# Two encoder layers on one core: products of probabilities placed one projection or a gate later, and the ring of PSUM banks begun at bank 7

## The chip, the cores and the metric

The kernel runs on one core of one Trainium2 chip. The metric is device time in microseconds (us) of one execution. The kernel before takes 1705.44 us, the median of 3 runs (1705.37 to 1705.56). PE is TensorE, DVE is VectorE, ACT is ScalarE, SP is SyncE, which issues the loads of the weights; PSUM has 8 banks of 128 x 512 floats here, named 0 to 7.

## The reference

An encoder of two layers over 512 tokens of 1024 channels in float32. Each layer computes

```
h = rmsnorm(x);  z = h @ w_in          # q, k, v of three mixers, and three gates
y_na  = neighbourhood attention of z   # 8 heads of 64, window 8 x 16 on a 64-wide grid
y_mla = latent attention of z          # 4 heads
y_gqa = windowed grouped attention     # 8 heads, 2 key heads, window 128, a sink logit
x = x + (sum_i sigmoid(gate_i) * (y_i @ w_br_i)) @ w_out
x = x + conv_ffn(rmsnorm(x))           # up to 2 x 2816, conv of width 3, gelu, down
```

and a last rmsnorm follows. Every attention is scores, softmax, and the product of the probabilities with the values.

## The kernel before, in words

Activations are held as [channel, token] tiles of 128 x 512. A float32 product is made of three fp32r matmuls: each operand is split into a high part (a cast by ACT, line 153) and a low part (the rest, by DVE, line 154), and `mm3` (lines 162 to 169) adds high x high, low x high and high x low. A projection of the 1024 channels (`dense`, line 171) is 8 x 3 = 24 matmuls of 128 x 512, a branch product (`do_br`, line 730) 4 x 3 = 12.

The order of PE and of SP is written out by hand: `schedule` (line 274) returns a list of items, and `run` (line 337) emits them one after the other. DVE and ACT are ordered by the framework's scheduler, which puts splits of weights and softmax work ahead by a priority. The engines take their instructions in that order. The items that matter here, `p` being a pair of heads, `h` a head, `i` a block of 128 queries of one key head:

- `("naq", p)`, `("nak", p)`, `("nav", p)`: projections for q, k, v of neighbourhood attention (24 matmuls each). `("nvt", p)` transposes v (4 matmuls, line 642).
- `("ns", p)`: scores of two heads into 4 banks; DVE adds the bias (line 674), finds maxima (line 677), ACT takes the exponential (line 679), DVE scales (line 682). `("nt", p)`: 32 small transposes of the probabilities into 4 banks (line 234), from which ACT casts `ph` and DVE subtracts `pl` (`unfold`, line 237). `("np", h)` (line 692): 8 matmuls of 256 columns of one head's `ph` and `pl` with the values (line 702); ACT and DVE then take the result from its bank (lines 706, 708).
- `("gs", i)`, `("gt", i)`, `("gp", i)`: the same three steps of the grouped-query mixer. The scores are masked by DVE (line 817); a block has 2 or 3 key blocks, so `gp` (lines 856 and 857) is 4 or 6 matmuls of 512 columns. There is a single pair of `ph` and `pl` buffers here.
- `gate()`: the next gate, 24 matmuls, evacuated by DVE into a `gz` tile (line 160; 5 buffers, line 39) and by ACT's tanh (line 718). `("br", b, m)`: a branch product, 12 matmuls, whose bank and gate DVE merges (lines 738, 740, 741).

The weights come as `raw` tiles (3 buffers, loaded by SP, line 118) and are split into `whi` and `wlo` (3 buffers each). When an item takes its weights, the split of the item two further on is emitted (`weights`, line 141), so that it starts when the item before has given its buffer back: a gate's weights are 128 x 1024, a branch product's 128 x 512.

Between the latent attention and the output projection all items take their banks in turn from one ring of eight (`do_mla_attn`, line 521, sets it; `bank`, line 104, hands them out). One layer takes 203 banks from it. Then `do_out` (line 871) sets groups: the first four output products run in banks 2, 3, 4, 5, the next in 6, 7, 0, 1.

Of the kernel before, what the change touches and what calls it, by code (L numbers as in the profile page):

```python
# [59 lines left out]
class Trunk:  # L60
# [213 lines left out]
    def schedule(self, l):  # L274
        d = self.d
        w_in, w_uq, w_ukv = d["w_in"][l], d["w_uq"][l], d["w_ukv"][l]
        W = {}
        halves = lambda w, cs: [(w, 512 * hf, 4, c, P) for hf in range(2) for c in cs]
        W["lat"] = halves(w_in, [OFF_CQ + i * P for i in LAT])
        if l == 0:  # L280
            W["lat"][:4] = [(w_in, k * P, 1, OFF_CQ, 4 * P) for k in range(4)]
        W["lat4"] = [(w_in, 0, KD, OFF_CQ + 4 * P, P)]
        W["kr"] = [(w_in, 0, KD, OFF_KR, 64)]
        W["v", 0] = [(w_ukv, 0, 2, 512, 512)]
        W["qr"] = [(w_uq, 0, 3, 512, 256)]
        for h in range(4):
            W["qn", h] = [(w_uq, 0, 3, h * P, P)]
            W["kn", h] = [(w_ukv, 0, 2, h * P, P)]
        for p in range(4):
            for i, n in enumerate("qkv"):  # L290
                W["na" + n, p] = [(w_in, 0, KD, 512 * i + p * P, P)]
        W["gk"] = [(w_in, 0, KD, OFF_GK, P)]
        W["gv"] = [(w_in, 0, KD, OFF_GV, P)]
        for i in range(4):
            W["gq", i] = [(w_in, 0, KD, OFF_GQ + i * P, P)]
        for b in range(3):
            for m in range(KD):
                W["gate", b, m] = [(w_in, 0, KD, OFF_GATE + b * D + m * P, P)]
                W["br", b, m] = [(d["w_br"][b][l], 0, 4, m * P, P)]
        W["br012"] = W["br", 2, 0] + W["br", 2, 1] + W["br", 2, 2]  # L300
        W["out"] = halves(d["w_out"][l], [m * P for m in range(4)])
        for m in range(4, KD):
            W["out", m] = [(d["w_out"][l], 0, KD, m * P, P)]
        ups = [p * NF + f for f in range(NF) for p in range(2)]
        W["up"] = halves(d["w_up"][l], [f * P for f in ups[:4]])
        for f in ups[4:]:
            W["up", f] = [(d["w_up"][l], 0, KD, f * P, P)]
        for g in range(2):
            W["down", g] = [(d["w_down"][l], k0 * P, nk, (4 * g + m) * P, P)
                            for k0, nk in ((0, 8), (8, 8), (16, 6)) for m in range(4)]  # L310

        gate = iter([("gate", b, m) for b in (1, 0, 2) for m in range(8)]).__next__
        s = ["mla_open", "lat", "qr", "lat4", "rs_q", "kr", gate(), "rs_k", ("qn", 0), ("v", 0), ("v", 1), "rb_k"]
        s += [("kn", 0), gate(), "mla_attn", ("qn", 1), ("kn", 1), ("mr", 0), ("ms", 0), gate()]
        for h in range(3):
            s += [("mt", h), ("mr", h + 1), ("ms", h + 1)]
            s += [("qn", h + 2), ("kn", h + 2)] if h < 2 else [("naq", 0)]
            s += [("mp", h)] + ([gate()] if h == 1 else [])
        s += [("nak", 0), ("mt", 3), gate(), ("nav", 0), ("mp", 3), "na_open", ("nvt", 0), ("ns", 0)]
        s += [("naq", 1), ("nak", 1), ("br", 1, 0), gate(), ("ns", 1), ("nt", 0)]  # L320
        s += [("nav", 1), ("np", 0), ("np", 1), ("naq", 2), ("nvt", 1), ("nak", 2), ("br", 1, 1), gate(), ("ns", 2), ("nt", 1)]
        s += [("nav", 2), ("np", 2), ("np", 3), ("naq", 3), ("nvt", 2), ("nak", 3), ("br", 1, 2), gate(), ("ns", 3), ("nt", 2)]
        s += [("nav", 3), ("np", 4), ("np", 5), ("br", 1, 3), gate(), ("nvt", 3), ("br", 1, 4), gate(), ("br", 1, 5), ("nt", 3)]
        s += [("br", 1, 6), gate(), ("np", 6), ("np", 7), ("br", 1, 7)]
        s += ["gq_open", "gk", ("gq", 0), "gv", ("gq", 1), "gvt", gate(), ("gs", 0), ("br", 0, 0), ("gq", 2), ("br", 0, 1), ("gq", 3)]
        for i in range(7):
            s += [("gs", i + 1), ("gt", i), ("br", 0, i + 1) if i else gate(), ("gp", i), gate()]
        s += [("gt", 7), gate(), ("gp", 7), "br012", ("br", 2, 3)]
        for m in range(4, 7):
            s += [gate(), ("br", 2, m)]  # L330
        s += [("br", 2, 7)]
        s += ["out"] + [("out", m) for m in range(4, KD)]
        s += ["up"] + [("up", f) for f in ups[4:]]
        s += [("down", 0), ("down", 1)]
        return s, W
# [183 lines left out]
            self.qr.append((own, other))  # L519

    def do_mla_attn(self):
        self.banks(ring=list(range(8)))

    def do_qn(self, h):
        ps = self.dense(self.spec(), self.lat[:3])
# [593 lines left out]
```

## Time and profile before

| | us |
|---|---|
| median of 3 runs | 1705.44 |
| the profiled execution | 1705.71 |
| its span, first to last instruction | 1703.9 |
| PE busy | 1684.3 |
| DVE busy | 1119.9 |
| ACT busy | 829.6 |
| PE's waits that the list of waits names | 14.4 |

The first layer's neighbourhood section lies at about 138 to 265 us of the span, its grouped-query section at 294 to 407, its output projection begins at 446; in the second layer the same sections lie at 982 to 1108, 1139 to 1251, and 1290 us. A row of the timeline reads: start, duration, engine, line, operation, tile written <- tiles read, size, count, and in brackets how long the engine had been idle before it and who ended that. A matmul's row lasts until the modelled end of its pipeline, so rows of matmuls that follow each other closely overlap: how fast they follow is read from their starts.

### The profile page before, as it was taken

Reading aid. Unit: us, or ns where it says so; the run is one execution under the profiler, and the core shown is the slowest. Engines: PE = TensorE matmul, PEld = TensorE weight load, DVE = VectorE, ACT = ScalarE, POOL = GpSimd, SP = SyncE. Lnnn points to the kernel's source line nnn. Section 1 sums busy time; section 2 is a strip of 40 time slices with the busy share of each in tenths; the row PEclk is TensorE's granted clock in tenths of the full one; section 3 lists DMA queues with packets and bytes.
Section 4 is the critical chain, followed back from the end, with each engine's and each line's share of the span. In section 5 each row is a group of like instructions: output and inputs, shape, how many; then the busy total and the mean of one; then the engine's idle time right before and its main releaser. Section 6 shows DMA issues by size and latency. Waiting matters only on the chain.

```text
span 1703.9 us, 22124 instructions
## 1 busy us (share of the span) xinstructions
PE 1684.3 (99%) x8466; PEld 1386.8 (81%) x8466; DVE 1119.9 (66%) x1845; ACT 829.6 (49%) x1461; POOL 52.2 (3%) x107
## 2 busy tenths in 40 slices
PE   9999999999999999999999999999999999999998
PEld 8887788878888888888887887887788888888887
DVE  7777766786558777734367687668766587777234
ACT  7654445675435444433266554467644444444232
POOL 1110000000000000000011100000000000000000
PEclk9999999999999999999999999999999999999999
DMA  6233223222324333323232323322223333333231
GB/s 183 68 102 85 78 84 88 74 69 75 105 83 116 98 100 99 99 87 101 80 96 80 96 75 84 90 81 69 64 79 105 99 112 98 93 94 99 87 105 68
DMA packets 289401, 155.44 MB, mean 91 GB/s; under 512 B 8880, under 2 KB 285376, under 8 KB 289296
## 3 DMA queue, kind: packets, MB, share of 16 engines
q1 hardware_dynamic: 286752, 148.88, 30.5%
q0 software_dynamic: 2256, 4.83, 0.9%
q8 instruction: 66, 1.08, 0.3%
q14 instruction: 39, 0.32, 0.1%
q10 hardware_dynamic: 288, 0.33, 0.1%
HBM read 151.89 MB, written 2.10 MB: 90 GB/s over the span
## 4 chain that ended last, share of the span: by engine, by line
PE 93%; DVE 5%; ACT 1%; issue 1%; DMA 0%; ACTq 0%
PE ps_ring L167 12%; PE ps_ring L168 11%; PE ps_ring L169 11%; PE ps_d L169 11%; PE ps_d L168 11%; PE ps_d L167 11%; PE ps_g L167 7%; PE ps_g L168 7%; PE ps_g L169 7%; DVE pl L154 1%; PE ps_ring L247 1%; PE ps_ring L234 1%; DVE wlo L154 1%; PE ps_ring L857 1%; PE ps_ring L702 1%; PE ps_g L267 1%
## 5 line engine op out<-in xcount | busy, mean ns | idle before, releaser
L153 ACT CAST whi<-raw 128x1024 fp32r<-128x1024 f32 (+4 forms) x339 | 301.0, 888 | 603.5 <-PE ps_g L168 190.5
L154 DVE TENSOR_TENSOR wlo<-raw,whi 128x1024 fp32r<-128x1024 f32 (+4 forms) x337 | 344.5, 1022 | 187.3 <-ACT whi L153 185.8
L169 PE MATMUL ps_d<-hh,wlo 128*128 128x512 f32 x685 | 266.7, 389 | 0.0
L168 PE MATMUL ps_d<-hl,whi 128*128 128x512 f32 x685 | 266.5, 389 | 0.0
L167 PE MATMUL ps_d<-hh,whi 128*128 128x512 f32 x685 | 266.5, 389 | 0.0
L167 PE MATMUL ps_ring<-hh,whi 128*128 128x512 f32 x600 | 234.8, 391 | 0.6 <-DVE pt L674 0.6
L169 PE MATMUL ps_ring<-hh,wlo 128*128 128x512 f32 x600 | 233.7, 389 | 0.0
L168 PE MATMUL ps_ring<-hl,whi 128*128 128x512 f32 x600 | 233.6, 389 | 0.0
L169 PEld LDWEIGHTS ps_d<-hh,wlo 128*128 128x128 f32 x685 | 128.6, 188 | 27.1 <-DVE wlo L154 0.6
L168 PEld LDWEIGHTS ps_d<-hl,whi 128*128 128x128 f32 x685 | 128.6, 188 | 26.7
L167 PEld LDWEIGHTS ps_d<-hh,whi 128*128 128x128 f32 x685 | 128.6, 188 | 26.6
L167 PEld LDWEIGHTS ps_ring<-hh,whi 128*128 128x128 f32 x600 | 112.7, 188 | 24.6 <-DVE pt L674 1.0
L169 PEld LDWEIGHTS ps_ring<-hh,wlo 128*128 128x128 f32 x600 | 112.6, 188 | 23.8
L168 PEld LDWEIGHTS ps_ring<-hl,whi 128*128 128x128 f32 x600 | 112.7, 188 | 23.2
L169 PE MATMUL ps_g<-ff,wlo 128*128 128x512 f32 x334 | 129.9, 389 | 0.0
L167 PE MATMUL ps_g<-ff,whi 128*128 128x512 f32 x334 | 129.9, 389 | 0.0
L168 PE MATMUL ps_g<-ff,whi 128*128 128x512 f32 x334 | 129.9, 389 | 0.0
L160 DVE TENSOR_TENSOR u<-ps_d,rb 128x512 f32<-128x512 f32 x80 | 55.2, 690 | 63.2 <-PE ps_d L169 63.2
L160 DVE TENSOR_TENSOR gz<-ps_ring,rb 128x512 f32<-128x512 f32 x44 | 30.4, 691 | 94.9 <-PE ps_ring L169 94.9
L167 PEld LDWEIGHTS ps_g<-ff,whi 128*128 128x128 f32 x334 | 62.7, 188 | 13.1
L169 PEld LDWEIGHTS ps_g<-ff,wlo 128*128 128x128 f32 x334 | 62.7, 188 | 13.0
L168 PEld LDWEIGHTS ps_g<-ff,whi 128*128 128x128 f32 x334 | 62.7, 188 | 12.9
(331 smaller groups left out, 2864.3 us busy)
## 6 DMA issues: line engine op xcount, KB each, us to landing
raw<-in_w_in_dram SPq DMA_DIRECT2D x86, 512.0 KB, 3.9
raw<-in_w_up_dram SPq DMA_DIRECT2D x80, 512.0 KB, 3.7
raw<-in_w_down_dram SPq DMA_DIRECT2D x32, 512.0 KB, 3.8
raw<-in_w_down_dram SPq DMA_DIRECT2D x16, 384.0 KB, 3.4
raw<-in_w_in_dram SPq DMA_DIRECT2D x17, 256.0 KB, 2.8
raw<-in_w_br_mla_dram SPq DMA_DIRECT2D x16, 256.0 KB, 2.7
raw<-in_w_br_na_dram SPq DMA_DIRECT2D x16, 256.0 KB, 2.7
raw<-in_w_br_gqa_dram SPq DMA_DIRECT2D x16, 256.0 KB, 2.8
```

Source lines behind the costliest of these rows:

```text
L153: nc.scalar.copy(hi, src)
L154: nc.vector.tensor_sub(lo, src, r32(hi))
L160: self.nc.vector.tensor_tensor(out, a, b, ALU.mult)
L167: mm(ps, sh, mh, start=first and k == 0, stop=False)
L168: mm(ps, sh, ml, start=False, stop=False)
L169: mm(ps, sl, mh, start=False, stop=last and k == n - 1)
L234: self.nc.tensor.transpose(out[i][:, n * 64:n * 64 + 64], block[q], self.idf[q, q])
L247: self.nc.tensor.matmul(out, st[a], mv[b], start=first and t == 0, stop=last and t == 2)
L267: self.nc.tensor.matmul(self.gbank[j], w[:, j * P:(j + 1) * P], m, start=n + t == 0, stop=False)
L702: nc.tensor.matmul(pq[:, qs], self.vs[p][:, ch, j, :], pm[:].rearrange("p (k c) -> p k c", c=P)[:, ks], start=i == 0 and m == 0, stop=i == ...
L857: nc.tensor.matmul(po, self.gvs[:, k0 + kb, g, :], pl, start=False, stop=kb == nk - 1)
```

## The change

Three things are changed: the place of `np` in the neighbourhood rows, the place of `gp` in the grouped-query loop, and the first bank of the ring.

```diff
-        s += [("nav", 1), ("np", 0), ("np", 1), ("naq", 2), ("nvt", 1), ("nak", 2), ("br", 1, 1), gate(), ("ns", 2), ("nt", 1)]
+        s += [("nav", 1), ("naq", 2), ("np", 0), ("np", 1), ("nvt", 1), ("nak", 2), ("br", 1, 1), gate(), ("ns", 2), ("nt", 1)]
...
-        s += [("nav", 3), ("np", 4), ("np", 5), ("br", 1, 3), gate(), ("nvt", 3), ("br", 1, 4), gate(), ("br", 1, 5), ("nt", 3)]
+        s += [("nav", 3), ("br", 1, 3), ("np", 4), ("np", 5), ("nvt", 3), gate(), ("br", 1, 4), gate(), ("br", 1, 5), ("nt", 3)]
...
-            s += [("gs", i + 1), ("gt", i), ("br", 0, i + 1) if i else gate(), ("gp", i), gate()]
+            s += [("gs", i + 1), ("gt", i), gate(), ("gp", i), ("br", 0, i + 1) if i else gate()]
...
     def do_mla_attn(self):
-        self.banks(ring=list(range(8)))
+        self.banks(ring=[7, 0, 1, 2, 3, 4, 5, 6])
```

The row that begins with `("nav", 2)` is changed like the first one: `("naq", 3)` goes ahead of `("np", 2)` and `("np", 3)`. For `i = 0` the loop's order stays as it was, with a gate on both sides of `gp`. The number of banks taken from the ring is the same 203.

On PE, in the first layer's loop at `i = 4`, behind the scores of block 5 and the transposes of block 4, a branch product stood ahead of `gp`; before:

```order
L247 MATMUL ps_ring<-gk,gq 128x384 x12
L234 MATMUL ps_ring<-idf,pt 128x64 x16
L167 MATMUL ps_ring<-ynh_1925,whi 128x512
L168 MATMUL ps_ring<-ynl_1926,whi 128x512
L169 MATMUL ps_ring<-ynh_1925,wlo 128x512
```

and now:

```order
L247 MATMUL ps_ring<-gk,gq 128x384 x12
L234 MATMUL ps_ring<-idf,pt 128x64 x16
L167 MATMUL ps_ring<-h_102,whi 128x512
L168 MATMUL ps_ring<-h_103,whi 128x512
L169 MATMUL ps_ring<-h_102,wlo 128x512
```

The tiles `ynh` and `ynl` are the neighbourhood mixer's output, which the branch product reads; `h` is the normed input, which the gate reads. The 12 matmuls between the transposes and `gp` have become 24, and the 12 now stand between `gp` and the next scores.

On DVE, at the same place, the queue behind PE's last item before the scores of block 5 (a gate before, a branch product now) up to the masked scores (`pt_3834` to `pt_3849`); before:

```order
L160 TENSOR_TENSOR gz_3814<-ps_ring_3789,rb_327 128x512
L154 TENSOR_TENSOR wlo_3885<-raw_3882,whi_3884 128x512
L817 ISA pt_3834,nm_3817<-ps_ring_3818,gmask_99,nsink_2875 128x384
L817 ISA nm_3817 128x1
L817 ISA pt_3837,nm_3817<-ps_ring_3819,gmask_99,nsink_2875 128x384
L817 ISA nm_3817 128x1
L817 ISA pt_3846,nm_3817<-ps_ring_3826,gmask_99,nsink_2875 128x384
L817 ISA nm_3817 128x1
L817 ISA pt_3849,nm_3817<-ps_ring_3827,gmask_99,nsink_2875 128x384
```

and now:

```order
L740 SCALAR_TENSOR_TENSOR gz_3357<-gz_3357,ps_ring_3802 128x512
L154 TENSOR_TENSOR yal0_3789<-yf_3360,yah0_3788 128x512
L741 TENSOR_TENSOR mg4_2656<-mg4_2656,gz_3357 128x512
L817 ISA pt_3834,nm_3817<-ps_ring_3818,gmask_99,nsink_2875 128x384
L817 ISA nm_3817 128x1
L817 ISA pt_3837,nm_3817<-ps_ring_3819,gmask_99,nsink_2875 128x384
L817 ISA nm_3817 128x1
L154 TENSOR_TENSOR wlo_3885<-raw_3882,whi_3884 128x1024
L817 ISA pt_3846,nm_3817<-ps_ring_3826,gmask_99,nsink_2875 128x384
L817 ISA nm_3817 128x1
L154 TENSOR_TENSOR yal1_3793<-yf_3360,yah1_3792 128x512
L817 ISA pt_3849,nm_3817<-ps_ring_3827,gmask_99,nsink_2875 128x384
```

In place of a gate's evacuation and a narrow `wlo` there stand the two instructions of a merge, a wide `wlo`, and (in this pass alone) the low parts `yal` of two finished output tiles. The two `pl` subtractions follow right behind the last row now; before, three small softmax instructions stood between.

On DVE in the neighbourhood section, behind the scaling of the probabilities of `("ns", 1)` (`pt_1810` is the last), the difference reads:

```order
 L682 TENSOR_SCALAR pt_1810<-pt_1810,nm_1812 128x256 x2
-L708 TENSOR_TENSOR yf_1541<-ps_ring_1913,tt_1922 64x4x8x16
-L154 TENSOR_TENSOR ynl0_1926<-yf_1541,ynh0_1925 128x512
-L160 TENSOR_TENSOR ev_1960<-ps_ring_1935,rb_327 128x512
+L160 TENSOR_TENSOR ev_1932<-ps_ring_1907,rb_327 128x512
 L154 TENSOR_TENSOR wlo_1978<-raw_1975,whi_1977 128x1024
+L154 TENSOR_TENSOR nq_1935<-ev_1932,nq_1934 128x512
+L708 TENSOR_TENSOR yf_1541<-ps_ring_1950,tt_1959 64x4x8x16
 L154 TENSOR_TENSOR vs_1966<-ps_ring_1967,vs_1966 128x8x64
-L154 TENSOR_TENSOR nq_1963<-ev_1960,nq_1962 128x512
+L708 TENSOR_TENSOR yf_1541<-ps_ring_1938,tt_1947 64x4x8x16
+L154 TENSOR_TENSOR ynl0_1963<-yf_1541,ynh0_1962 128x512
```

The evacuation (`ev`) and split (`nq`) of the next q projection have moved ahead of the evacuation (`yf`) of the two `np` products and of the split of their sum.

More of the change, by code (lines that the diff above doesn't have):

```diff
@@ L320, in schedule @@
         s += [("naq", 1), ("nak", 1), ("br", 1, 0), gate(), ("ns", 1), ("nt", 0)]
-        s += [("nav", 1), ("np", 0), ("np", 1), ("naq", 2), ("nvt", 1), ("nak", 2), ("br", 1, 1), gate(), ("ns", 2), ("nt", 1)]
-        s += [("nav", 2), ("np", 2), ("np", 3), ("naq", 3), ("nvt", 2), ("nak", 3), ("br", 1, 2), gate(), ("ns", 3), ("nt", 2)]
-        s += [("nav", 3), ("np", 4), ("np", 5), ("br", 1, 3), gate(), ("nvt", 3), ("br", 1, 4), gate(), ("br", 1, 5), ("nt", 3)]
+        s += [("nav", 1), ("naq", 2), ("np", 0), ("np", 1), ("nvt", 1), ("nak", 2), ("br", 1, 1), gate(), ("ns", 2), ("nt", 1)]
+        s += [("nav", 2), ("naq", 3), ("np", 2), ("np", 3), ("nvt", 2), ("nak", 3), ("br", 1, 2), gate(), ("ns", 3), ("nt", 2)]
+        s += [("nav", 3), ("br", 1, 3), ("np", 4), ("np", 5), ("nvt", 3), gate(), ("br", 1, 4), gate(), ("br", 1, 5), ("nt", 3)]
         s += [("br", 1, 6), gate(), ("np", 6), ("np", 7), ("br", 1, 7)]
```

## The prediction

> **What bounds the kernel now.** I read the page first, then PE's list of waits, then the timeline at each wait, of PE and of the engine waited for.
>
> ```profile
> span 1703.9 us, 22124 instructions
> PE 1684.3 (99%) x8466; PEld 1386.8 (81%) x8466; DVE 1119.9 (66%) x1845; ACT 829.6 (49%) x1461; POOL 52.2 (3%) x107
> ```
>
> PE is busy for 99% of the span, so nothing but PE's stalls can be won, some 20 us at most. The profiled execution took 1705.71 us, 1.8 us more than its span and 0.27 us more than the median of the runs, 1705.44. Terms come from the profiled one and are taken off the median. PE's waits, in us in total, times, and the longest:
>
> ```profile
> PE ps_ring L702 <- DVE pl L154: 5.8, 4, 1.4
> PE ps_ring L857 <- DVE pl L154: 3.8, 10, 0.6
> PE ps_g L167 <- DVE gz L740: 1.7, 2, 0.9
> PE ps_ring L167 <- DVE pt L674: 1.2, 6, 0.2
> ```
>
> The first two are products of probabilities that wait for DVE's low part `pl`: line 702 in neighbourhood attention, line 857 in the grouped-query loop. The third is the first output product, which waits for DVE to empty a bank. The three come to 11.3 us, and the change touches each. The fourth is the bank of the first projection behind `nt`; that projection keeps its place and its bank's history, so I leave it.
>
> These figures are idle time behind a matmul's modelled end, and a stall costs more. So I price each stall by whole sections, from first start to next start, against the same section where nothing waits.
>
> **Neighbourhood rows.** The stalled pair of `np` in the first layer, then a pair that has no stall:
>
> ```profile
> 167.85 0.28 PE L702 MATMUL ps_ring<-ph,vs 128*128 128x256 f32 x1
> 170.57 0.39 PE L702 MATMUL ps_ring<-pl,vs 128*128 128x256 f32 x1 [1.45 <-DVE pl L154]
> 171.50 0.39 PE L167 MATMUL ps_ring<-h,whi 128*128 128x512 f32 x1
> 176.97 0.60 PE L642 MATMUL ps_ring<-idf,vt 128*128 128x128 f32 x4
> 231.38 0.28 PE L702 MATMUL ps_ring<-ph,vs 128*128 128x256 f32 x1
> 233.30 0.39 PE L167 MATMUL ps_ring<-yah,whi 128*128 128x512 f32 x1
> ```
>
> Stalled, 16 matmuls take 171.50 - 167.85 = 3.65 us; unstalled 233.30 - 231.38 = 1.92 us. A stall costs 1.73 us, and there are four (the wait's count): 6.9 us.
>
> In the changed order the q projection runs first. It takes 176.97 - 171.50 = 5.47 us, so `np` begins at 167.85 + 5.47 = 173.3. Its operand and what PE needs next are ready by then:
>
> ```profile
> 169.24 1.28 DVE L154 TENSOR_TENSOR pl<-ps_ring,ph 128x512 fp32r<-128x512 f32 x2
> 170.82 1.13 DVE L160 TENSOR_TENSOR vt<-ps_ring,rb 128x448 f32<-128x448 f32 x2
> ```
>
> The last `pl` ends at 170.52, 2.8 us ahead. The transposes of v, now right behind `np` at 173.3 + 1.9 = 175.2, need `vt`, which ends at 171.95. The q projection's bank is now the second score bank, the first two `np` products get the third and fourth; all were read by DVE before `pl`. The two products' results wait longer on DVE, behind `ev` and `nq`, since `ev` and the copy `tt` share a buffer; their banks come round again only at the scores of the next pair, a projection, a branch product and a gate later (some 13 us). I cost that at nothing. The row of `("nav", 3)` has no stall to lose, and its branch product needs nothing new: nothing.
>
> **Grouped-query loop.** The stalled product at `i = 4` and PE's items ahead of it, `i = 1` and `i = 6` (first and last stalled of six), and the unstalled `i = 0`:
>
> ```profile
> 363.17 1.31 PE L247 MATMUL ps_ring<-gk,gq 64*128 64x384 f32 x12
> 367.82 0.50 PE L856 MATMUL ps_ring<-ph,vs 128*128 128x512 f32 x1
> 368.92 0.50 PE L857 MATMUL ps_ring<-pl,vs 128*128 128x512 f32 x1 [0.60 <-DVE pl L154]
> 369.71 0.39 PE L167 MATMUL ps_ring<-h,whi 128*128 128x512 f32 x1
> ...
> 331.94 0.40 PE L856 MATMUL ps_ring<-ph,vs 128*128 128x512 f32 x1
> 333.98 0.39 PE L167 MATMUL ps_ring<-h,whi 128*128 128x512 f32 x1
> ...
> 392.48 0.40 PE L856 MATMUL ps_ring<-ph,vs 128*128 128x512 f32 x1
> 394.14 0.39 PE L167 MATMUL ps_ring<-h,whi 128*128 128x512 f32 x1
> ...
> 320.48 0.39 PE L856 MATMUL ps_ring<-ph,vs 128*128 128x512 f32 x1
> 321.40 0.39 PE L167 MATMUL ps_ring<-h,whi 128*128 128x512 f32 x1
> ```
>
> Unstalled, 4 matmuls take 0.92 us, 0.23 each, so 6 take 1.38. The six take 2.04, 1.81, 1.73, 1.89, 2.03 and 1.66 us, four of them with 6 matmuls: 11.16 against 4 x 1.38 + 2 x 0.92 = 7.36. That is 3.8 us per layer, 7.6 in both. (The list names 10 waits, not 12: at `i = 6` the stall is too short to leave PE idle behind the modelled end.)
>
> What goes in between is a gate in place of a branch product: 12 matmuls more. A full-width matmul follows the last in 5.47 / 24 = 0.228 us, so `pl` is needed 2.73 us later than now. But DVE also has more to do first. Its queue at `i = 4` now, and ACT's cast ahead of the wide split:
>
> ```profile
> 361.64 1.29 DVE L154 TENSOR_TENSOR yal<-yf,yah 128x512 fp32r<-128x512 f32 x2 [0.69 <-ACT yah L153]
> 363.27 0.69 DVE L160 TENSOR_TENSOR gz<-ps_ring,rb 128x512 f32<-128x512 f32 x1 [0.34 <-PE ps_ring L169]
> 363.88 0.68 DVE L154 TENSOR_TENSOR wlo<-raw,whi 128x512 fp32r<-128x512 f32 x1
> 364.48 0.61 DVE L817 CUSTOM_DVE_ANT_0 pt<-ps_ring,gmask,nsink 128x384 f32<-128x384 f32 x1
> 366.09 0.61 DVE L817 CUSTOM_DVE_ANT_0 pt<-ps_ring,gmask,nsink 128x384 f32<-128x384 f32 x1
> 367.58 1.28 DVE L154 TENSOR_TENSOR pl<-ps_ring,ph 128x512 fp32r<-128x512 f32 x2
> 368.78 0.68 DVE L740 SCALAR_TENSOR_TENSOR gz<-gz,ps_ring 128x512 f32<-128x512 f32 x1
> 370.83 1.23 DVE L154 TENSOR_TENSOR wlo<-raw,whi 128x1024 fp32r<-128x1024 f32 x1
> 369.75 1.04 ACT L153 CAST whi<-raw 128x1024 fp32r<-128x1024 f32 x1
> ```
>
> Start to start, a full-width DVE instruction takes 0.6 us, a mask 0.54 (364.48 to 366.09 is three), the wide `wlo` some 1.15. In the new queue, from the same start at 363.27: merge 2 x 0.6 (line 741 adds what line 740 made), `yal` 2 x 0.6, four masks 2.15, wide `wlo` 1.15, two `pl` 1.2 + 0.1. That is 7.0, so `pl` is ready at 370.3. It is needed at 367.82 + 0.23 + 2.73 = 370.8. So the pass with the most work has 0.5 us to spare. The other five lack the 1.2 us of `yal`; four of them have one `pl` more (0.6), so they spare at least 1.1 us, with `i = 3` at 1.7 (four more transposes on PE and narrower masks, not counted, add to it). ACT's wide cast, 1.04 us from the moment the branch product gives its buffer back, ends about when the merge does; at `i = 4` two masks stand in between as well.
>
> Other waits that the order could bring. The merge stood behind `pl` and now stands first, which frees the branch product's bank and `gz` buffer early; five gates are alive at once now, in five buffers, and the one needed was merged a pass before. `gp`'s single buffers are free a branch product, scores and transposes ahead of the next `ph`, instead of a gate: still over 4 us. SP's loads change places in pairs, a gate's 512 KB ahead of a branch product's 256 KB. All of it at nothing; its price if the cover fails is in the rivals.
>
> **Rotation of the ring.**
>
> ```profile
> 444.71 0.39 PE L169 MATMUL ps_ring<-yah,wlo 128*128 128x512 f32 x1
> 445.97 0.47 PE L167 MATMUL ps_g<-mo,whi 128*128 128x512 f32 x1 [0.87 <-DVE gz L740]
> ```
>
> A layer takes 203 banks, 25 x 8 + 3, so the last branch product has the ring's third bank: bank 2, where the first output product begins. It waits until DVE has read it: 445.97 - 444.71 - 0.23 = 1.03 us, twice 2.1. With the ring begun at 7 the third bank is 1. Banks 2 to 5 were then last used by `("br", 2, 3)` and the gates and branch product behind it, and bank 1 serves the eighth output product. At the ring's start each item gets the neighbour's bank, none of them emptied later than the one it had. Gain 2.1 us.
>
> **The sum.** 6.9 + 7.6 + 2.1 = 16.6 us. 1705.44 - 16.6 = 1688.8 us. What is next late is the fourth wait of the list (1.2 us), unchanged. Whether PE keeps its clock when it stalls less is shown by a stretch without stalls:
>
> ```profile
> 450.00:880.00 430.00, 430.00 (x1902) 355.96 (x1901) 255.31 (x326) 175.02 (x231) 8.92 (x12) 1.00 0.34 99
> ```
>
> 430 us at full granted clock (1.00).
>
> The idle rows alone would have given 11.3 us. The Trainium skill, TensorE: Matmul & The Clock Gate, under "Single matmul latency" and "Back-to-back issue gap", has a lone matmul at (398 + N)/2.4 ns and a following one at N/2.4 + 2.5, so that each interrupted stream also pays the pipeline's drain, 163 ns. The trace agrees (0.39 us a row, 0.228 from start to start), and by an estimate from that page the sum would be 11.3 + 16 x 0.163 = 13.9 us, 1691.5. The whole sections give more, since the second matmul behind a stall is late too, and the sections decide.
>
> **The rivals.** About 0.2% (3.4 us) is what a measurement of this kernel can tell from no change.
>
> A. Only what the list of waits names comes back: 1705.44 - 11.3 = 1694.1 us. For it: the idle rows are what the profile calls waiting. Against it: unstalled sections of the same matmuls stand in the same trace, and are shorter by the full amount. 3%.
>
> B. DVE hands `pl` over late in the grouped-query loop after all, since in its queue the wide split, behind ACT's cast, now stands ahead of the masks. For it: 0.5 us to spare at `i = 4`. If those two products still wait about as long as now, 2 x 0.97 comes off, 1690.7; if DVE is later by the full 2.73 us in every pass, all 7.6, 1696.4. Against it: the other passes spare over 1 us. 10%. The same page, under "Architectural detail", calls ACT's and DVE's queues strict first in, first out, which speaks against this change: the masks can't pass a split that waits. The trace agrees, `pl` at 367.58 standing behind masks and small softmax steps.
>
> C. Slower: the wide split at the head of DVE's queue waits for its load in every pass. The page has such a load at
>
> ```profile
> raw<-in_w_in_dram SPq DMA_DIRECT2D x86, 512.0 KB, 3.9
> ```
>
> 3.9 us to landing. Held by that, `pl` comes 3.9 - 1.5 = 2.4 us late in twelve passes: 29 us, 1718 us. It decides from 1.5 + 16.6 / 12 = 2.9 us of hold per pass. Against it: with three buffers a load starts when the split three before is done, and a pass of 12 us has two splits, so it has some 18 us. 3%.
>
> D. The rotation only moves its wait: 2.1 us stay, 1690.9. Against it: the count of banks above. 2%.
>
> E. The stalls go, and PE loses as much at places not seen here: about 1705. Nothing in the trace speaks for it. 2%.
>
> **How the numbers follow.** The forecast, all three waits gone, has 80%, with 1687.8 to 1690.0 as its own range (half a microsecond or one of small stalls left, or half the fourth wait gone). A, B, D are faster too: faster 0.95. E is no change: 0.02. C is slower: 0.03. The range goes from 1687.5 up to 1692.5, which takes in D and the likelier half of B and leaves out A, the rest of B, C and E.
>
> **What would show it.** Right: line 702 gone from PE's waits, line 857 gone or under 1 us, the output's first product without a wait, `gp` at 0.92 or 1.38 us and `np` at 1.92, line 674's 1.2 us still there. Wrong: a wait at line 857 for `pl`, first at `i = 4` (B); DVE idle ahead of a wide `wlo` for a load (C); a wait of the output product or of the items behind the ring's start for a bank (D).

## The result and the profile after

The changed kernel takes 1688.87 us, the median of 4 runs (1688.39 to 1689.73), beside 1705.5 us (1705.37 to 1705.87) for the kernel before. The ratio is 0.9903, with a 95% interval of 0.9886 to 0.9920: faster by 16.6 us, about 1%. The forecast was 1688.8 us. The profiled execution took 1688.89 us.

The head of the page of the changed kernel:

```profile
span 1687.1 us, 22130 instructions
PE 1678.7 (100%) x8466; PEld 1388.2 (82%) x8466; DVE 1119.5 (66%) x1845; ACT 832.5 (49%) x1461; POOL 51.8 (3%) x107
```

The span is 16.8 us shorter, with the same 8466 matmuls. PE's own busy time fell by 5.6 us though no matmul went: a matmul just behind a stall has a longer row (0.50 for 0.39 us), and rows that overlap are counted once. Busy time and idle time each hold a part of a stall. All of PE's waits that the list names in the changed kernel (total, times, longest):

```profile
PE idle L361 <- DVE cst L85: 1.0, 1, 1.0
PE ps_ring L167 <- DVE pt L674: 1.0, 6, 0.2
PE ps_ring L247 <- DVE gq L154: 0.6, 2, 0.3
PE ps_ring L642 <- DVE vt L160: 0.5, 2, 0.3
```

Lines 702 and 857 are gone, and so is the output's wait for `gz`. The wait at line 674 stays, as forecast (1.0 us for 1.2). The last line is new and was not forecast: PE's transposes of v (line 642) wait for DVE's copy `vt`.

The first neighbourhood pair now. The first row is its first matmul, the second the transposes behind it:

```profile
173.46 0.28 PE L702 MATMUL ps_ring<-ph,vs 128*128 128x256 f32 x1
...
175.37 0.60 PE L642 MATMUL ps_ring<-idf,vt 128*128 128x128 f32 x4
```

16 matmuls take 175.37 - 173.46 = 1.91 us; they took 3.65. Next the pass at `i = 4`, the one with the least to spare, on DVE and on PE:

```profile
358.18 0.69 DVE L740 SCALAR_TENSOR_TENSOR gz<-gz,ps_ring 128x512 f32<-128x512 f32 x1 [0.52 <-PE ps_ring L169]
...
361.06 1.22 DVE L154 TENSOR_TENSOR wlo<-raw,whi 128x1024 fp32r<-128x1024 f32 x1
...
363.34 0.61 DVE L817 CUSTOM_DVE_ANT_0 pt<-ps_ring,gmask,nsink 128x384 f32<-128x384 f32 x1
...
363.88 1.28 DVE L154 TENSOR_TENSOR pl<-ps_ring,ph 128x512 fp32r<-128x512 f32 x2
...
365.39 0.39 PE L856 MATMUL ps_ring<-ph,vs 128*128 128x512 f32 x1
365.62 0.39 PE L857 MATMUL ps_ring<-pl,vs 128*128 128x512 f32 x1
...
366.31 0.39 PE L167 MATMUL ps_ring<-ynh,whi 128*128 128x512 f32 x1
```

The last `pl` ends at 365.16, 6.98 us behind the merge's start (forecast 7.0), and PE reads the first at 365.62: 0.46 us to spare (forecast 0.5). The product takes 366.31 - 365.39 = 0.92 us, unstalled. At the output, PE's last branch product and the first output product:

```profile
437.67 0.39 PE L169 MATMUL ps_ring<-yah,wlo 128*128 128x512 f32 x1
437.89 0.39 PE L167 MATMUL ps_g<-mo,whi 128*128 128x512 f32 x1
```

They follow each other in 0.22 us, where 1.26 us lay between.

Where the time came from is read from the starts of the same sections in both timelines (first matmul of each, in us):

| start of | layer 1 before | after | difference | layer 2 before | after | difference |
|---|---|---|---|---|---|---|
| first neighbourhood scores | 138.49 | 138.66 | +0.17 | 982.46 | 974.18 | -8.28 |
| first grouped-query scores | 294.84 | 291.74 | -3.10 | 1138.80 | 1127.26 | -11.54 |
| last grouped-query product | 405.92 | 398.87 | -7.05 | 1249.89 | 1234.38 | -15.51 |
| output projection | 445.97 | 437.89 | -8.08 | 1289.95 | 1273.40 | -16.55 |

Each difference less the one above it is a section's gain. The neighbourhood rows gave 3.27 and 3.26 us, the grouped-query loop 3.95 and 3.97, the stretch to the output 1.03 and 1.04. The remaining 0.3 us of the 16.8 by which the span is shorter is spread over the rest.

### The profile page after: what moved, and what is told of

The parts are those of the page before. It is cut to its first block, busy times and chain, and to the rows that moved or that the text cites. A ratio compares the mean times of both kernels' runs of the same rounds, so it can differ in the third digit from the quotient of the medians.

```text
span 1687.1 us, 22130 instructions
## 1 busy us (share of the span) xinstructions
PE 1678.7 (100%) x8466; PEld 1388.2 (82%) x8466; DVE 1119.5 (66%) x1845; ACT 832.5 (49%) x1461; POOL 51.8 (3%) x107
## 4 chain that ended last, share of the span: by engine, by line
PE 97%; DVE 2%; ACT 0%; issue 0%; ACTq 0%
PE ps_ring L167 13%; PE ps_ring L168 12%; PE ps_ring L169 12%; PE ps_d L169 11%; PE ps_d L168 11%; PE ps_d L167 11%; PE ps_g L168 7%; PE ps_g L167 7%; PE ps_g L169 7%; PE ps_ring L247 2%; PE ps_ring L234 1%; PE ps_g L267 1%; PE ps_ring L702 1%; PE ps_ring L857 1%; PE ps_ring L856 1%; DVE wlo L154 1%
```

## The experiments

The first four ran on one chip, beside 13 runs of the kernel before (median 1705.61 us, 1705.15 to 1706.46); the other four on another chip, beside 7 runs (1706.26, 1705.92 to 1708.12).

**Each part alone.** The first kernel is the kernel before with the three neighbourhood rows of the changed one:

```diff
-        s += [("nav", 1), ("np", 0), ("np", 1), ("naq", 2), ("nvt", 1), ...]
+        s += [("nav", 1), ("naq", 2), ("np", 0), ("np", 1), ("nvt", 1), ...]
...
-        s += [("nav", 3), ("np", 4), ("np", 5), ("br", 1, 3), gate(), ("nvt", 3), ...]
+        s += [("nav", 3), ("br", 1, 3), ("np", 4), ("np", 5), ("nvt", 3), gate(), ...]
```

> The kernel before with the neighbourhood rows alone changed. Sections add (mine): the four stalled pairs of products go from 3.65 to 1.92 us, 6.9 us less, and the value transposes of the third row cost 0.4 us a layer, 0.9 in all, so some 6.0 us less than before, 1699.4 us; the grouped-query stalls and the output's 1.03 us wait stay as before. Rival, only the listed waits come back: 5.8 less 0.5, some 5.3 us, 1700.1. Rival, the parts hide each other's stalls: a stall saved here comes back at the grouped-query loop, under 3 us less.

It took 1699.10 us (1698.98 to 1699.36), ratio 0.9962 [0.9947, 0.9976]: 6.5 us less. Among PE's waits in it:

```profile
PE ps_ring L857 <- DVE pl L154: 3.8, 10, 0.6
PE ps_g L167 <- DVE gz L740: 1.7, 2, 0.9
...
PE ps_ring L642 <- DVE vt L160: 0.5, 2, 0.3
```

Line 702 is gone, the other two waits are whole, and the new wait for `vt` is there: it belongs to this part of the change.

The second is the kernel before with the loop's line alone:

```diff
-            s += [("gs", i + 1), ("gt", i), ("br", 0, i + 1) if i else gate(), ("gp", i), gate()]
+            s += [("gs", i + 1), ("gt", i), gate(), ("gp", i), ("br", 0, i + 1) if i else gate()]
```

> The kernel before with the grouped-query loop alone changed. Sections add (mine): 7.6 us less than before (2 x 3.8), 1697.9 us, every product at 0.92 or 1.38 us; neighbourhood stalls (line 702) and the output's wait stay. Rival, only the listed waits come back: 3.8 us less, 1701.7. Rival, the parts hide each other's stalls: under 3 us less.

It took 1697.64 us (1697.32 to 1699.73), ratio 0.9955 [0.9941, 0.9970]: 8.0 us less. PE's two longest waits in it:

```profile
PE ps_ring L702 <- DVE pl L154: 5.8, 4, 1.4
PE ps_g L167 <- DVE gz L740: 1.7, 2, 0.9
```

Line 857 is gone. The list had given it 3.8 us, and 8.0 came back, so the idle rows undercount by half here.

The third is the kernel before with the ring's line alone:

```diff
-        self.banks(ring=list(range(8)))
+        self.banks(ring=[7, 0, 1, 2, 3, 4, 5, 6])
```

> The kernel before with the ring of banks alone begun at bank 7. Sections add (mine): 2.1 us less than before, 1703.4 us, the first output product without a wait, all other waits as before. Rival, only the listed waits come back: 1.7 us less. Rival, the wait moves to another bank: 0 us less.

It took 1703.61 us (10 runs, 1703.15 to 1705.21), ratio 0.9989 [0.9979, 0.9998]: 2.0 us less. Its list keeps lines 702 and 857 at 5.8 and 3.8 us, and has no output wait. A wait of 0.3 us at line 234 is new in it. The kernel with the transposes behind the gate (below) has that wait in one of its two profiles and not in the other, so it is not shown that the rotation causes it.

For the first and the third part the intervals, some 2 us to either side, don't tell what came back from the listed idle time alone (5.3 and 1.7 us in the rivals). The starts of the rows do: the stalled pairs take 1.91 us in the first kernel, for 3.65, and in the third the first output product follows 0.23 us behind the last branch product, for 1.26. The three parts give 6.5 + 8.0 + 2.0 = 16.5 us, the whole change 16.6: they add up, and nothing shows that one gives back what another wins.

**The new wait for `vt`.** In the changed kernel the transposes of v go back behind a gate, in the third row:

```diff
-        s += [("nav", 3), ("br", 1, 3), ("np", 4), ("np", 5), ("nvt", 3), gate(), ("br", 1, 4), ...]
+        s += [("nav", 3), ("br", 1, 3), ("np", 4), ("np", 5), gate(), ("nvt", 3), ("br", 1, 4), ...]
```

> The changed kernel with the value transposes of the third row put back behind the gate. Mine: the wait for vt (0.43 us in each layer by the starts of the rows) goes, 0.8 us less than the changed kernel, 1688.0 us, and nothing else moves. Rival, the wait is not set by the transposes' place (the scaling on VectorE holds up the next item whatever it is): the same time as the changed kernel, 1688.9.

It took 1688.24 us (1687.63 to 1689.39), ratio 0.9899 [0.9884, 0.9913]. The new wait is gone from its list, but the changed kernel was not among these four, and a gain under 1 us can't be told across chips. So both were run side by side:

> The changed kernel once more, beside the next one on one chip: 1688.9 us.

> The changed kernel with the value transposes of the third row behind the gate, once more, beside the changed kernel on one chip. Mine: 0.8 us less than it (0.39 in each layer in the stretch from the third pair of scores to the grouped-query section). Rival, the start of the execution and not the transposes made the difference of the first comparison: the same time.

The changed kernel took 1689.38 us (1688.76 to 1689.49; ratio 0.9901 [0.9886, 0.9915]), the one with the transposes behind the gate 1688.25 (1688.08 to 1688.36; ratio 0.9895 [0.9880, 0.9909]). No run of the one reaches the other, but the two intervals overlap, and 1.1 us is more than the wait can explain. PE's rows of the latter, the end of the third pair, and the transposes at their new place:

```profile
230.03 0.28 PE L702 MATMUL ps_ring<-ph,vs 128*128 128x256 f32 x1
...
231.95 0.40 PE L167 MATMUL ps_ring<-h,whi 128*128 128x512 f32 x1
...
237.42 0.60 PE L642 MATMUL ps_ring<-idf,vt 128*128 128x128 f32 x4
237.77 0.48 PE L167 MATMUL ps_ring<-yah,whi 128*128 128x512 f32 x1
```

The pair takes 231.95 - 230.03 = 1.92 us again, and the transposes pass in 0.35 us without a wait. From the third row's `np` to the next section each layer takes 60.73 us for 61.11, 0.38 less. So the wait is worth 0.8 us; the rest of the 1.1 us is of the size by which executions differ at the program's start (last section). By its medians this is the fastest version of the study.

**How near the grouped-query loop is to DVE's limit.** In the changed kernel two of the four masks of each block are computed twice, with the same result written again, which gives DVE two masks more to compute in each pass, in most of them ahead of `pl`:

```diff
-                nc.vector.tensor_tensor_reduce(pt[:, :w], sp[hh], self.gmask[:, m0:m0 + w], -HD_SCALE,
...
+                for _ in range(2 if hh < 2 else 1):
+                    nc.vector.tensor_tensor_reduce(pt[:, :w], sp[hh], self.gmask[:, m0:m0 + w], -HD_SCALE,
...
```

> The changed kernel with two of the four masks of every block of scores computed twice on VectorE: 0.8 to 1.1 us more work ahead of the last low part in most passes (in the pass of block 4 the repeats fall behind it), 15 us more VectorE work in all. Mine: only the pass i = 4, with 0.46 us to spare in the changed kernel's trace, stalls, by 0.6 us in each layer; i = 5, with 1.07 to spare, at the edge; 1.3 to 1.7 us more than the changed kernel, 1690.4. Rival, VectorE has become the bound of the loop: 15 us more, 1704. Rival, a first in, first out queue with no room anywhere: every pass stalls, 6 to 8 us more.

It took 1691.32 us (1690.92 to 1692.80), ratio 0.9914 [0.9899, 0.9929]: 1.9 us more than the changed kernel beside it. The line number of the product of `pl` is 858 here. The waits' line, and the rows at `i = 0` and `i = 4`:

```profile
PE ps_ring L858 <- DVE pl L154: 1.3, 2, 0.6
```

```profile
318.73 0.40 PE L857 MATMUL ps_ring<-ph,vs 128*128 128x512 f32 x1
319.14 0.50 PE L858 MATMUL ps_ring<-pl,vs 128*128 128x512 f32 x1
...
359.82 0.69 DVE L740 SCALAR_TENSOR_TENSOR gz<-gz,ps_ring 128x512 f32<-128x512 f32 x1 [0.22 <-PE ps_ring L169]
...
367.32 0.68 DVE L154 TENSOR_TENSOR pl<-ps_ring,ph 128x512 fp32r<-128x512 f32 x1
...
367.03 0.40 PE L857 MATMUL ps_ring<-ph,vs 128*128 128x512 f32 x1
368.06 0.50 PE L858 MATMUL ps_ring<-pl,vs 128*128 128x512 f32 x1 [0.63 <-DVE pl L154]
368.39 0.39 PE L857 MATMUL ps_ring<-ph,vs 128*128 128x512 f32 x1
368.62 0.40 PE L858 MATMUL ps_ring<-pl,vs 128*128 128x512 f32 x1
```

At `i = 4` DVE needs 368.00 - 359.82 = 8.18 us, 1.20 more than in the changed kernel; 0.46 were spare, and PE starts the second product 1.03 us behind the first, for 0.23. At `i = 0` it is 0.41, too short for the list. By stretches the two passes lose 0.91 and 0.28 us in each layer, 2.4 in both, of which the medians show 1.9. They are the two with the least to spare in the changed kernel, 0.46 and 0.95 us; the others, with 1.07 or more, lose nothing (`i = 5` keeps 0.26 us; at `i = 3` the repeats fall behind `pl`, and its 1.74 stay whole). The expectation missed this in part: it had `i = 4` alone, at 0.6 us, with `i = 5` at the edge, and overlooked `i = 0`. DVE's busy time rose by 14.5 us (1119.6 to 1134.1), the kernel's time by 1.9. So PE still sets the time of this loop, and added DVE work costs only what a pass has not to spare.

**Another rotation.** The changed kernel with the ring begun at 1:

```diff
-        self.banks(ring=[7, 0, 1, 2, 3, 4, 5, 6])
+        self.banks(ring=[1, 2, 3, 4, 5, 6, 7, 0])
```

> The changed kernel with the ring begun at bank 1 in place of bank 7. The last branch product then has bank 3, which the second output product takes 2.7 us later, and the one before it bank 2, emptied 2 us before it is taken. Mine: the same time as with 7, 1688.9 us, and no wait at the output product. Rival, the direction or the particular bank 7 matters: the output's wait is back, 2.1 us more.

It took 1689.10 us (1688.95 to 1690.07), ratio 0.9901 [0.9885, 0.9918]: the same as with 7. The output's first product follows the last branch product at once here too:

```profile
437.82 0.39 PE L169 MATMUL ps_ring<-yah,wlo 128*128 128x512 f32 x1
438.05 0.39 PE L167 MATMUL ps_g<-mo,whi 128*128 128x512 f32 x1
```

Seven is nothing special; what counts is that the last branch product's bank is not the output's first. Its list has one new line, at the ring's start in one layer, where a product takes the bank that DVE has just emptied of a gate:

```profile
PE ps_ring L247 <- DVE gz L160: 0.3, 1, 0.3
```

## Why the prediction was right, step by step

**What bounds the kernel.** Right: what was won were PE's stalls, and PE kept its clock. Only the cap, "some 20 us at most", was read from PE's idle time alone, and of the 16.8 us by which the span fell 5.6 came out of PE's busy time; it was no cap. The stretch between the two layers' attention in the changed kernel (the number ahead of the last two is the granted clock):

```profile
446.00:876.00 430.00, 430.00 (x1904) 355.92 (x1904) 258.62 (x331) 178.51 (x238) 9.21 (x14) 1.00 0.34 99
```

It is 1.00, as before.

**Neighbourhood pairs, 6.9 us.** Right: no stall is left at line 702, and each of the four pairs takes 1.91 us, for 3.64 to 3.66. That is 7.0 us. The whole section gave less, 3.27 + 3.26 = 6.5 us, since the third row took 0.8 back (next paragraph). The other items of the section gave 0.4 that was not forecast, each a few hundredths: 32 transposes, for one, take 1.32 us for 1.36, a q projection 5.44 for 5.47.

**The row of `("nav", 3)`, "nothing".** This step failed. In the changed kernel the third pair, then the transposes, and what DVE did meanwhile:

```profile
230.61 0.28 PE L702 MATMUL ps_ring<-ph,vs 128*128 128x256 f32 x1
...
232.95 0.63 PE L642 MATMUL ps_ring<-idf,vt 128*128 128x128 f32 x4 [0.27 <-DVE vt L160]
...
228.97 2.17 DVE L682 TENSOR_SCALAR pt<-pt,nm 128x256 f32<-128x256 f32 x8
231.06 0.97 DVE L160 TENSOR_TENSOR vt<-ps_ring,rb 128x448 f32<-128x448 f32 x1
231.95 0.69 DVE L154 TENSOR_TENSOR wlo<-raw,whi 128x512 fp32r<-128x512 f32 x1
232.55 0.25 DVE L160 TENSOR_TENSOR vt<-ps_ring,rb 128x64 f32<-128x64 f32 x1
```

PE is through with the pair at 230.61 + 1.92 = 232.53; `vt` ends at 232.80, and the transposes start at 232.95. The section takes 2.34 us for 1.91, 0.43 lost in each layer. I had asked only whether the branch product that moved ahead needs anything new, and had checked `vt` in the first row, where it ends in time. In the third row the transposes also came nearer: a gate (and a branch product) stood between `np` and them, and nothing does now. The trace of before already held what they would meet there:

```profile
232.48 2.17 DVE L682 TENSOR_SCALAR pt<-pt,nm 128x256 f32<-128x256 f32 x8
234.57 0.96 DVE L160 TENSOR_TENSOR vt<-ps_ring,rb 128x448 f32<-128x448 f32 x1
...
236.03 0.27 DVE L160 TENSOR_TENSOR vt<-ps_ring,rb 128x64 f32<-128x64 f32 x1
```

These are DVE's rows of the kernel before. In this row eight scalings stand ahead of `vt`, and it ends at 236.30, 4.92 us behind the end of the v projection (231.38). The new order leaves it a branch product and the pair, 2.73 + 1.92 = 4.65 us. It is short by 0.27 us, which is just the idle time measured. The experiment that moves the transposes back behind a gate removed the wait and the loss.

**Grouped-query loop, 7.6 us.** Right: by the starts of their rows the products take 0.92 or 1.38 us in every pass, 3.8 us less in each layer. The sections gave a little more, 3.95 + 3.97 = 7.9 us, and the loop alone 8.0: the branch products also became shorter, at `i = 4` from 2.91 to 2.83 us. The sum of DVE's queue at `i = 4`, 7.0 us with 0.5 to spare, held to 0.04 us, and the repeated masks show that this slack, and not some other, decides.

**Rotation, 2.1 us.** Right: 1.03 + 1.04 us by sections, 2.0 alone.

**The sum.** 16.6 forecast, 16.6 measured by medians. That it fits this well is partly luck. By the starts of the rows the three terms came out as priced: 7.0, 7.6 and 2.1 us. But the 0.8 us lost in the third row had no term, and it was made up by gains that had none either: 0.4 in the other items of the neighbourhood section, 0.3 in the loop (its branch products above all), 0.3 in the rest. Why those items became shorter is not shown.

**The rivals.** A, the idle rows alone (11.3 us), falls: the loop alone gave 8.0 for its 3.8 idle. B, a late `pl`, falls: 0.46 us were spare, and the masks show what it would have taken. That `pl` stands behind the masks in the traces is the order in which they were issued; no run here tests whether DVE could let one pass. C, a wide split that waits for its load, falls: `wlo` at 361.06 has no idle time before it, and neither has any other wide split of the loop in either layer. D, a rotation that only moves its wait, falls with both rotations. E, losses elsewhere, holds for 0.8 us.

By the Trainium skill's figures (TensorE: Matmul & The Clock Gate, under "Single matmul latency" and "Back-to-back issue gap") the estimate was 13.9 us; the measured 16.6 decides against it. Their figures for 512 columns come to 379 and 216 ns by estimate (the first is given for bf16) and lie 3 and 5% under the 0.39 and 0.228 us here, so they agree only roughly. The drain of 163 ns by the Trainium skill's estimate fits: a held matmul starts about 0.17 us later than its idle time says (last section). What the estimate leaves out are the second matmul behind each stall, late by 0.10 us, and the stalls at `i = 6`, which the list does not name (1.66 for 1.38 us in each layer).

## What to carry to other kernels

Price a stall by the same section where nothing waits, from start to start: the idle time that the list of waits shows was 11.3 us here, and the rows of the stalled sections became 16.6 us shorter. When an order is rewritten, ask of every item whose neighbours change what it reads and when that is ready in that very row, not in a row like it; an item that lost the work in front of it is as much moved as the one that was written elsewhere. Where cover is thin, count the other engine's queue instruction by instruction in the fullest pass, since 0.46 us of slack was told from a stall that way.

## What the runs showed of the hardware

A stall costs more than its idle time in two ways, seen in the rows at `i = 4` with the masks repeated. 1.03 us pass from the product of `ph` to the held one, 0.80 more than the usual 0.23, of which 0.63 is listed as idle. And the next matmul follows 0.33 us behind the held one (368.06 to 368.39), for 0.23. So 0.63 us idle cost 0.90.

The start of the program varies from execution to execution. The first product in a `ps_d` bank of four profiled executions, of the changed kernel, of it again, with the transposes behind the gate, and with the masks repeated, which do the same work up to there, starts at 27.71, 27.66, 27.09 and 28.31 us. So medians of kernels that differ by under 1 us hold some of this, and the stretches between section starts tell such differences better.
